# Row sums of a 64 MB array: the first 256 rows get a stretch of their own, and one semaphore guards the last store

## The chip, the core and the metric

The kernel runs on one core of a Trainium2 chip. The metric is the device time of one execution in microseconds (us), as the median over repeated runs. The engines that matter are DVE (VectorE), ACT (ScalarE), POOL (GpSimd) and SP (SyncE, which here issues every DMA); 16 DMA engines move the data. TensorE does no arithmetic here.

## The reference

```python
def setup_inputs():
    batch, seq, dim = 32, 512, 1024
    return {
        "x": np.random.randn(batch, seq, dim).astype(np.float32),
        "divisor": float(dim),
    }

def reference(x, divisor):
    return (np.sum(x, axis=-1) / divisor).astype(np.float32)
```

So x is 16,384 rows of 1,024 float32 (4 KB a row, 67.1 MB in all), and the output is one float32 per row, 64 KB.

## The kernel before

The rows are spread over the 128 partitions of the on-chip memory, 128 rows per partition. Three stretches of x are told apart, each with its own pattern of addresses. `x_first` is the start of x: 128 x 15 rows, where partition p owns 15 rows that follow one another, so that the whole stretch is packed. Behind it every partition owns W = 113 consecutive rows: the first M = 97 of them are `x_main`, the last L = 16 are `x_last`. Neighbouring partitions stand 113 rows (452 KiB) apart there.

The loads go, in this order, into three buffers `bulk0` to `bulk2` in turn (rows per partition, and in brackets how many of them ACT sums; DVE sums the others):

| load | 0 | 1 to 5 | 6 | 7 | 8 | 9 | then |
|---|---|---|---|---|---|---|---|
| stretch | main | main | main | first | last | last | last |
| rows | 2 (0) | 16 (0) each | 15 (4) | 15 (6) | 10 (4) | 4 (1) | 2, as `pa` and `pb` |

The lists in the code are `main = [(2, 0)] + [(16, 0)] * 5 + [(15, 4)]`, `first = [(15, 6)]` and `last = [(10, 4), (4, 1)]`. The last two rows come as `pa` (one and a half rows, 768 KB) and `pb` (half a row, 256 KB), so that little is left to add when the last bytes land.

DVE sums a load of `main` or `first` with one `reduce_sum` (L189), unscaled; ACT adds its rows one by one, with an activation that also gives the row's sum (L164). For `last`, DVE adds the two halves of a row with one custom instruction that scales and sums as well (`both_halves`, L180), and ACT scales in its activation. POOL scales the sums of `main` (L152) and `first` (L156) by 1/divisor afterwards. Sums stand in `res` (main), `res0` (first) and `fin` (last), and each of the three is stored by a DMA of its own.

The order is written out by hand. SP's first three loads (L111) are moved ahead of the program's opening barrier by `start_loads_at_once`. Each later bulk load (L138) waits until DVE and ACT are done with the buffer that it will overwrite, and until the load before it in that buffer has landed (L137). Then follow `pa` (L140) and `pb` (L141), the store of `res` (L143, after POOL's scaling), the store of `res0` (L145, likewise), and at the very end the store of `fin` (L205), which waits for ACT's count of rows and for DVE's count of instructions, two semaphores. The queue then waits for the two earlier stores, clears the semaphores (L210) and waits for the last store to land (L211). All DMAs stand in one queue, in the order of issue.

Of the kernel before, what the change touches and what calls it, by code (L numbers as in the profile page):

```python
# [9 lines left out]
COPY = mybir.ActivationFunctionType.Copy  # L10
# [24 lines left out]
@with_exitstack  # L35
def kernel(
    ctx: ExitStack,
    tc: tile.TileContext,
    x: bass.AP,
    divisor: float,  # L40
    out: bass.AP,
):
    nc = tc.nc
    nc.at_finalize(start_loads_at_once)
    xf = x.flatten_outer_dims()
    N, D = xf.shape
    P = nc.NUM_PARTITIONS
    scale = 1.0 / float(divisor)
    J = N // P
    assert J * P == N  # L50

    F, L = 15, 16
    M = J - F - L
    W = M + L
    x_first = bass.AP(tensor=x.tensor, offset=0, ap=[[F * D, P], [D, F], [1, D]])
    x_main = bass.AP(tensor=x.tensor, offset=P * F * D, ap=[[W * D, P], [D, M], [1, D]])
    x_last = bass.AP(tensor=x.tensor, offset=P * F * D + M * D, ap=[[W * D, P], [D, L], [1, D]])
    o_first = bass.AP(tensor=out.tensor, offset=0, ap=[[F, P], [1, F]])
    o_main = bass.AP(tensor=out.tensor, offset=P * F, ap=[[W, P], [1, M]])
    o_last = bass.AP(tensor=out.tensor, offset=P * F + M, ap=[[W, P], [1, L]])  # L60

    def room(name, *shape):
        return nc.alloc_sbuf_tensor(name, [P, *shape], F32).ap()


    base = -(-nc.sbuf_base // 32) * 32
    room("pad", -base % 1024 // 4)
    assert nc.sbuf_base % 1024 == 0
    c = 512
    bulk = [room(f"bulk{i}", r, D) for i, r in enumerate((16, 16, 16))]  # L70
    pa = room("pa", D + c)
    pb = room("pb", D - c + 16)[:, : D - c + 2]
    res0 = room("res0", F)
    res = room("res", M)
    fin = room("fin", L)
    junk = [nc.alloc_psum_tensor(f"junk{i}", [P, D], F32).ap() for i in range(4)]

    loads = []  # L80
    sems = {}

    def sem(name):
        sems[name] = nc.alloc_semaphore(name)
        return sems[name]

    in_bulk = [sem(f"in_bulk{i}") for i in range(3)]
    in_pa, in_pb = (sem(f"in_{n}") for n in ("pa", "pb"))
    out_first, out_main = sem("out_first"), sem("out_main")
    dve, act, pool = sem("by_dve"), sem("by_act"), sem("by_pool")  # L90
    landed = nc.alloc_semaphore("landed")

    n = 0
    main = [(2, 0)] + [(16, 0)] * 5 + [(15, 4)]
    first = [(15, 6)]
    last = [(10, 4), (4, 1)]
    assert sum(r for r, _ in first) == F
    assert sum(r for r, _ in main) == M and sum(r for r, _ in last) == L - 2
    for part, src, dst, by in (
        (main, x_main, res, 1.0), (first, x_first, res0, 1.0), (last, x_last, fin, scale)  # L100
    ):
        j = 0
        for rows, on_act in part:
            t, s, slot = bulk[n % 3][:, :rows, :], in_bulk[n % 3], n
            n += 1
            loads.append((t, s, src[:, j : j + rows, :], on_act, dst[:, j : j + rows], by, slot))
            j += rows


    for t, s, src, *_ in loads[:3]:  # L110
        i = nc.sync.dma_start(out=t, in_=src).then_inc(s, 16)  # L111
        tc.no_tile_sem_insts.add(i.ins.name)
    tc.close()
    tc.compile()  # L114


    done_dve, done_act = {}, {}
    d = a = 0
    for k, (t, s, src, on_act, dst, by, slot) in enumerate(loads):
        rows = t.shape[1]  # L120
        d += 1 if by == 1.0 else rows - on_act
        a += on_act
        done_dve[k], done_act[k] = d, a
    arrived, seen = [], {}
    for t, s, *_ in loads:
        seen[s.num] = seen.get(s.num, 0) + 16
        arrived.append(seen[s.num])


    for k, (t, s, src, on_act, dst, by, slot) in enumerate(loads):  # L130
        if k < 3:
            continue
        if slot is not None:
            nc.sync.wait_ge(dve, done_dve[k - 3])
            if done_act[k - 3]:
                nc.sync.wait_ge(act, done_act[k - 3])
            nc.sync.wait_ge(s, arrived[k] - 16)  # L137
        nc.sync.dma_start(out=t, in_=src).then_inc(s, 16)  # L138
    x_two = bass.AP(tensor=x.tensor, offset=x_last.offset + (L - 2) * D, ap=[[W * D, P], [1, 2 * D]])
    nc.sync.dma_start(out=pa, in_=x_two[:, : D + c]).then_inc(in_pa, 16)  # L140
    nc.sync.dma_start(out=pb[:, : D - c], in_=x_two[:, D + c :]).then_inc(in_pb, 16)  # L141
    nc.sync.wait_ge(pool, 2)
    nc.sync.dma_start(out=o_main, in_=res).then_inc(out_main, 16)  # L143
    nc.sync.wait_ge(pool, 3)
    nc.sync.dma_start(out=o_first, in_=res0).then_inc(out_first, 16)  # L145


    nc.gpsimd.memset(pb[:, D - c :], 0.0).then_inc(pool)  # L148
    k = len(main) - 1
    nc.gpsimd.wait_ge(dve, done_dve[k])  # L150
    nc.gpsimd.wait_ge(act, done_act[k])
    nc.gpsimd.tensor_scalar_mul(out=res, in0=res, scalar1=scale).then_inc(pool)  # L152
    k += len(first)
    nc.gpsimd.wait_ge(act, done_act[k])
    nc.gpsimd.wait_ge(dve, done_dve[k])
    nc.gpsimd.tensor_scalar_mul(out=res0, in0=res0, scalar1=scale).then_inc(pool)  # L156


    a = 0

    def row_on_act(src, by, dst):
        if a >= len(junk):
            nc.scalar.wait_ge(act, a - len(junk) + 1)
        nc.scalar.activation(junk[a % len(junk)], src, COPY, scale=by, accum_out=dst).then_inc(act)  # L164

    for k, (t, s, src, on_act, dst, by, slot) in enumerate(loads):
        rows = t.shape[1]
        for r in range(rows - on_act, rows):
            if r == rows - on_act:
                nc.scalar.wait_ge(s, arrived[k])  # L170
            row_on_act(t[:, r, :], by, dst[:, r : r + 1])
            a += 1
    nc.scalar.wait_ge(in_pa, 16)
    row_on_act(pa[:, :D], scale, fin[:, L - 2 : L - 1])
    a += 1


    def both_halves(dst, src, by):
        h = src.shape[-1] // 2
        return nc.vector.tensor_tensor_reduce(  # L180
            out=src[:, :h], in0=src[:, :h], in1=src[:, h:], scale=by, scalar=0.0,
            op0=ADD, op1=ADD, accum_out=dst,
        )

    for k, (t, s, src, on_act, dst, by, slot) in enumerate(loads):
        m = t.shape[1] - on_act
        nc.vector.wait_ge(s, arrived[k])
        if by == 1.0:
            nc.vector.reduce_sum(out=dst[:, :m], in_=t[:, :m, :], axis=AX).then_inc(dve)  # L189
        else:  # L190
            for r in range(m):
                both_halves(dst[:, r : r + 1], t[:, r, :], by).then_inc(dve)
    nc.vector.wait_ge(in_pa, 16)
    nc.vector.wait_ge(pool, 1)
    both_halves(pb[:, D - c : D - c + 1], pa[:, D:], 1.0).then_inc(dve)
    d += 1
    nc.vector.wait_ge(in_pb, 16)
    nc.vector.wait_ge(dve, d)
    both_halves(fin[:, L - 1 :], pb, scale).then_inc(dve)
    d += 1  # L200


    nc.sync.wait_ge(act, a)
    nc.sync.wait_ge(dve, d)
    nc.sync.dma_start(out=o_last, in_=fin).then_inc(landed, 16)  # L205
    for s in (out_first, out_main):
        nc.sync.wait_ge(s, 16)
    ids = [s.num for s in sems.values()]
    assert max(ids) - min(ids) + 1 == len(ids)
    nc.sync.sem_clear(range(min(ids), max(ids) + 1))  # L210
    nc.sync.wait_ge(landed, 16).then_inc(landed, -16)  # L211
# [35 lines left out]
```

## Time and profile before

| | |
|---|---|
| median of 3 runs | 160.44 us (160.41 to 160.47) |
| the profiled execution | 160.41 us, of which the traced span is 159.1 us |
| DVE busy | 116.5 us (73%) |
| ACT busy | 18.5 us (12%) |
| POOL busy | 1.0 us (1%) |
| DMA queue | 2160 packets, 67.18 MB, 98.1% of 16 engines' span, mean 422 GB/s |

The profile is of one execution. In the timeline a line gives start, duration, engine, source line and operation, and in brackets how long the engine had been idle and what ended that. A DVE or ACT line whose idle time ended with a DMA tells when that load landed. In the table of windows each line is a stretch of time with the busy time of DVE, ACT and POOL, the granted TensorE clock, the mean busy share of the DMA engines and GB/s; packets are counted where they start, so a short window can show more than the engines can move. In the table of DMA issues the last number is the time from issue to landing.

### The profile page before, as it was taken

The numbers are of one execution on the slowest core, as the hardware profiler recorded it, in microseconds if no ns is written. First come the engines' busy times: TensorE is split into PE (matmuls) and PEld (weight loads), VectorE is DVE, ScalarE is ACT, GpSimd is POOL, SyncE is SP. The second block draws the span as 40 slices with busy tenths as digits, with TensorE's granted clock in tenths as the row PEclk, the third lists the DMA queues.
The fourth block names the chain that finished last, engine by engine and source line by source line (L and its number), as shares of the span: only waits on it lengthen the run. The fifth ranks groups of instructions, "written<-read, shape, count | busy, mean of one in ns | idle before, by whom it ended". The sixth has DMA issues, their size and how long they took to land.

```text
span 159.1 us, 141 instructions
## 1 busy us (share of the span) xinstructions
DVE 116.5 (73%) x30; ACT 18.5 (12%) x33; POOL 1.0 (1%) x7
## 2 busy tenths in 40 slices
DVE  0500009999499994999949999599989990399475
ACT  3000000000000000000000000000009100392384
POOL 0000000000000000000000000000000001000000
DMA  8996996996997989969969969959996999798994
GB/s 330 461 527 264 527 527 264 527 527 264 527 478 313 527 363 428 527 264 527 527 264 527 527 264 527 494 247 494 494 494 278 463 494 494 330 453 371 420 400 152
DMA packets 2160, 67.18 MB, mean 422 GB/s; under 512 B 624, under 2 KB 624, under 8 KB 880
## 3 DMA queue, kind: packets, MB, share of 16 engines
q1 hardware_dynamic: 2160, 67.18, 98.1%
HBM read 67.11 MB, written 0.07 MB: 422 GB/s over the span
## 4 chain that ended last, share of the span: by engine, by line
DMA 67%; DVE 29%; another core or an unknown queue 1%; ACT 1%; SPq 1%; issue 0%
DMA bulk<-in_x_dram 51%; DVE res L189 29%; DMA pa<-in_x_dram 15%; ACT junk L164 1%; SPq L111 1%; SPq L138 0%
## 5 line engine op out<-in xcount | busy, mean ns | idle before, releaser
L189 DVE TENSOR_REDUCE res<-bulk 128x16 f32<-128x16384 f32 (+3 forms) x8 | 110.0, 13753 | 37.4 <-DMA bulk<-in_x_dram 37.4
L164 ACT ACTIVATE junk<-bulk 128x1024 f32<-128x1024 f32 x15 | 15.2, 1012 | 136.0 <-DMA bulk<-in_x_dram 136.0
L180 DVE CUSTOM_DVE_ANT_0 bulk<-bulk 128x512 f32<-128x512 f32 x9 | 5.7, 689 | 3.4 <-DMA bulk<-in_x_dram 3.4
L164 ACT ACTIVATION_READ_ACCUMULATOR junk<-bulk 128x1 f32 x15 | 2.8, 187 | 0.0
L164 ACT ACT_TABLE_LOAD x1 | 1.3, 1283 | 2.4 <-PEq L114 2.4
L152 POOL TENSOR_SCALAR res<-res 128x97 f32<-128x97 f32 x1 | 0.5, 465 | 128.9 <-DVE res L189 128.9
L164 ACT ACTIVATE junk<-pa 128x1024 f32<-128x1024 f32 x1 | 1.0, 1028 | 0.7 <-DMA pa<-in_x_dram 0.7
L180 DVE DVE_READ_ACCUMULATOR2_ANT fin<- 128x1 f32 x10 | 0.8, 83 | 0.0
L180 DVE CUSTOM_DVE_ANT_0 pb<-pb 128x257 f32<-128x257 f32 x1 | 0.4, 429 | 0.3 <-DMA pb<-in_x_dram 0.3
L180 DVE CUSTOM_DVE_ANT_0 pa<-pa 128x256 f32<-128x256 f32 x1 | 0.4, 426 | 0.0
L156 POOL TENSOR_SCALAR res<-res 128x15 f32<-128x15 f32 x1 | 0.3, 263 | 15.7 <-DVE res L189 15.7
L164 ACT ACTIVATION_READ_ACCUMULATOR junk<-pa 128x1 f32 x1 | 0.2, 186 | 0.0
L148 POOL MEMSET pb<- 128x2 f32 x1 | 0.1, 99 | 2.0 <-POOLq L114 2.0
L228 POOL MEMSET const-bfloat16-1.0<- 128x1 bf16 x1 | 0.1, 101 | 0.0
L228 POOL MEMSET const-uint8-127<- 128x1 uint8 x1 | 0.1, 101 | 0.0
L228 POOL MEMSET const-float32-0.0<- 128x1 f32 x1 | 0.1, 99 | 0.2 <-issue 0.2
L228 POOL MEMSET const-float32-1.0<- 128x1 f32 x1 | 0.1, 98 | 0.0
L180 DVE DVE_READ_ACCUMULATOR2_ANT pb<- 128x1 f32 x1 | 0.1, 83 | 0.0
## 6 DMA issues: line engine op xcount, KB each, us to landing
bulk<-in_x_dram SPq DMA_DIRECT2D x2, 7680.0 KB, 38.9
bulk<-in_x_dram SPq DMA_DIRECT2D x1, 5120.0 KB, 31.1
bulk<-in_x_dram SPq DMA_DIRECT2D x1, 2048.0 KB, 23.2
bulk<-in_x_dram SPq DMA_DIRECT2D x1, 1024.0 KB, 4.6
pa<-in_x_dram SPq DMA_DIRECT2D x1, 768.0 KB, 24.6
pb<-in_x_dram SPq DMA_DIRECT2D x1, 256.0 KB, 24.9
bulk<-in_x_dram SPq DMA_DIRECT2D x5, 40.8
out_dram<-res SPq DMA_DIRECT2D x1, 48.5 KB, 24.6
```

The lines of the kernel that those rows point to most:

```text
L111: i = nc.sync.dma_start(out=t, in_=src).then_inc(s, 16)
L148: nc.gpsimd.memset(pb[:, D - c :], 0.0).then_inc(pool)
L152: nc.gpsimd.tensor_scalar_mul(out=res, in0=res, scalar1=scale).then_inc(pool)
L156: nc.gpsimd.tensor_scalar_mul(out=res0, in0=res0, scalar1=scale).then_inc(pool)
L164: nc.scalar.activation(junk[a % len(junk)], src, COPY, scale=by, accum_out=dst).then_inc(act)
L180: return nc.vector.tensor_tensor_reduce(out=src[:, :h], in0=src[:, :h], in1=src[:, h:], scale=by, scalar=0.0, op0=ADD, op1=ADD, accum_out=dst,
L189: nc.vector.reduce_sum(out=dst[:, :m], in_=t[:, :m, :], axis=AX).then_inc(dve)
L228: nc = _bacc.Bacc("TRN2", target_bir_lowering=False, num_devices=1)
```

## The change

A fourth stretch, `x_begin`, is cut off the start of x: G = 2 rows per partition, 256 rows, packed in 1 MB. It takes the place of the two rows of `main` that were loaded first; `first` (15 rows per partition, packed) follows it in memory, and `main` and `last` are now 95 + 16 = 111 rows per partition. The order and the sizes of the loads remain: 2, five times 16, 15, 15, 10, 4 rows, `pa`, `pb`.

The two rows of `begin` are summed on DVE by `both_halves`, scaled at once, into a tile of their own, `res1`, which gets a store of its own, issued right after that of `res0`. POOL scales 95 columns of `res` in place of 97.

A semaphore `done` counts the last instruction of ACT and the last of DVE; the last store waits for it alone to reach 2. The queue's closing waits take in the new store.

```diff
-    F, L = 15, 16
-    M = J - F - L
+    G, F, L = 2, 15, 16
+    M = J - G - F - L
     W = M + L
-    x_first = bass.AP(tensor=x.tensor, offset=0, ap=[[F * D, P], [D, F], [1, D]])
-    x_main = bass.AP(tensor=x.tensor, offset=P * F * D, ap=[[W * D, P], [D, M], [1, D]])
+    x_begin = bass.AP(tensor=x.tensor, offset=0, ap=[[G * D, P], [D, G], [1, D]])
+    x_first = bass.AP(tensor=x.tensor, offset=P * G * D, ap=[[F * D, P], [D, F], [1, D]])
+    x_main = bass.AP(tensor=x.tensor, offset=P * (G + F) * D, ap=[[W * D, P], [D, M], [1, D]])
...
+    o_begin = bass.AP(tensor=out.tensor, offset=0, ap=[[G, P], [1, G]])
...
+    res1 = room("res1", G)
     res = room("res", M)
...
-    main = [(2, 0)] + [(16, 0)] * 5 + [(15, 4)]
+    begin = [(2, 0)]
+    main = [(16, 0)] * 5 + [(15, 4)]
...
-        (main, x_main, res, 1.0), (first, x_first, res0, 1.0), (last, x_last, fin, scale)
+        (begin, x_begin, res1, scale), (main, x_main, res, 1.0),
+        (first, x_first, res0, 1.0), (last, x_last, fin, scale),
...
     nc.sync.dma_start(out=o_first, in_=res0).then_inc(out_first, 16)
+    nc.sync.dma_start(out=o_begin, in_=res1).then_inc(out_begin, 16)
...
-    row_on_act(pa[:, :D], scale, fin[:, L - 2 : L - 1])
-    a += 1
+    row_on_act(pa[:, :D], scale, fin[:, L - 2 : L - 1], done)
...
-    both_halves(fin[:, L - 1 :], pb, scale).then_inc(dve)
-    d += 1
-    nc.sync.wait_ge(act, a)
-    nc.sync.wait_ge(dve, d)
+    both_halves(fin[:, L - 1 :], pb, scale).then_inc(done)
+    nc.sync.wait_ge(done, 2)
     nc.sync.dma_start(out=o_last, in_=fin).then_inc(landed, 16)
-    for s in (out_first, out_main):
+    for s in (out_begin, out_first, out_main):
         nc.sync.wait_ge(s, 16)
```

More of the change, by code (lines that the diff above doesn't have):

```diff
@@ L50 @@
     assert J * P == N
-    F, L = 15, 16
-    M = J - F - L
+    G, F, L = 2, 15, 16
+    M = J - G - F - L
     W = M + L
-    x_first = bass.AP(tensor=x.tensor, offset=0, ap=[[F * D, P], [D, F], [1, D]])
-    x_main = bass.AP(tensor=x.tensor, offset=P * F * D, ap=[[W * D, P], [D, M], [1, D]])
[L57 to L60, printed above, removed]
+    x_begin = bass.AP(tensor=x.tensor, offset=0, ap=[[G * D, P], [D, G], [1, D]])
+    x_first = bass.AP(tensor=x.tensor, offset=P * G * D, ap=[[F * D, P], [D, F], [1, D]])
+    x_main = bass.AP(tensor=x.tensor, offset=P * (G + F) * D, ap=[[W * D, P], [D, M], [1, D]])
+    x_last = bass.AP(tensor=x.tensor, offset=P * (G + F) * D + M * D, ap=[[W * D, P], [D, L], [1, D]])
+    o_begin = bass.AP(tensor=out.tensor, offset=0, ap=[[G, P], [1, G]])
+    o_first = bass.AP(tensor=out.tensor, offset=P * G, ap=[[F, P], [1, F]])
+    o_main = bass.AP(tensor=out.tensor, offset=P * (G + F), ap=[[W, P], [1, M]])
+    o_last = bass.AP(tensor=out.tensor, offset=P * (G + F) + M, ap=[[W, P], [1, L]])
     def room(name, *shape):
@@ L88 @@
     in_pa, in_pb = (sem(f"in_{n}") for n in ("pa", "pb"))
-    out_first, out_main = sem("out_first"), sem("out_main")
+    out_begin, out_first, out_main = (sem(f"out_{n}") for n in ("begin", "first", "main"))
     dve, act, pool = sem("by_dve"), sem("by_act"), sem("by_pool")
+    done = sem("done")
     landed = nc.alloc_semaphore("landed")
     n = 0
-    main = [(2, 0)] + [(16, 0)] * 5 + [(15, 4)]
+    begin = [(2, 0)]
+    main = [(16, 0)] * 5 + [(15, 4)]
     first = [(15, 6)]
@@ L145 @@
     nc.sync.dma_start(out=o_first, in_=res0).then_inc(out_first, 16)
+    nc.sync.dma_start(out=o_begin, in_=res1).then_inc(out_begin, 16)
     nc.gpsimd.memset(pb[:, D - c :], 0.0).then_inc(pool)
-    k = len(main) - 1
+    k = len(begin + main) - 1
     nc.gpsimd.wait_ge(dve, done_dve[k])
@@ L159, with row_on_act @@
     a = 0
-    def row_on_act(src, by, dst):
+    def row_on_act(src, by, dst, count):
         if a >= len(junk):
             nc.scalar.wait_ge(act, a - len(junk) + 1)
-        nc.scalar.activation(junk[a % len(junk)], src, COPY, scale=by, accum_out=dst).then_inc(act)
+        nc.scalar.activation(junk[a % len(junk)], src, COPY, scale=by, accum_out=dst).then_inc(count)
     for k, (t, s, src, on_act, dst, by, slot) in enumerate(loads):
@@ L170 @@
                 nc.scalar.wait_ge(s, arrived[k])
-            row_on_act(t[:, r, :], by, dst[:, r : r + 1])
+            row_on_act(t[:, r, :], by, dst[:, r : r + 1], act)
             a += 1
     nc.scalar.wait_ge(in_pa, 16)
-    row_on_act(pa[:, :D], scale, fin[:, L - 2 : L - 1])
-    a += 1
+    row_on_act(pa[:, :D], scale, fin[:, L - 2 : L - 1], done)
     def both_halves(dst, src, by):
```

## The prediction

> **What bounds the kernel now.** I read the page first, then the timeline for the moments at which loads land, then windows over the start, then the end of the timeline and the queue's own waits. The page:
>
> ```profile
> span 159.1 us, 141 instructions
> DVE 116.5 (73%) x30; ACT 18.5 (12%) x33; POOL 1.0 (1%) x7
> q1 hardware_dynamic: 2160, 67.18, 98.1%
> DMA 67%; DVE 29%; another core or an unknown queue 1%; ACT 1%; SPq 1%; issue 0%
> ```
>
> The transfers are busy 98.1% of the span on one queue. The chain of waits names DVE for 29%, but that share is misleading: a chain followed back from the end may pass through a reduction that merely frees a buffer for a load that then stands in line. The timeline settles it:
>
> ```profile
> 0.00 1.32 SPq L111 DMA_DIRECT2D bulk<-in_x_dram  x3
> 4.65 2.29 DVE L189 TENSOR_REDUCE res<-bulk 128x2 f32<-128x2048 f32 x1 [4.65 <-DMA bulk<-in_x_dram]
> 6.96 124.72 SPq L138 DMA_DIRECT2D bulk<-in_x_dram  x7
> 23.95 17.22 DVE L189 TENSOR_REDUCE res<-bulk 128x16 f32<-128x16384 f32 x1 [17.02 <-DMA bulk<-in_x_dram]
> 43.29 17.22 DVE L189 TENSOR_REDUCE res<-bulk 128x16 f32<-128x16384 f32 x1 [2.12 <-DMA bulk<-in_x_dram]
> ...
> 119.44 11.89 DVE L189 TENSOR_REDUCE res<-bulk 128x11 f32<-128x11264 f32 x1 [0.90 <-DMA bulk<-in_x_dram]
> ...
> 137.66 9.75 DVE L189 TENSOR_REDUCE res<-bulk 128x9 f32<-128x9216 f32 x1 [6.33 <-DMA bulk<-in_x_dram]
> ```
>
> Every reduction waits for its load, never the other way round. From 4.65 to 119.44 five loads of 16 rows and one of 15 land: 95 rows per partition in 114.79 us, 1.208 us a row. A row of all partitions is 128 x 4096 = 524,288 bytes, so this is 434 GB/s. The packed load of 15 rows (119.44 to 137.66) needs 18.22 us, 1.215 us a row. With three buffers the queue always holds a load in waiting, and a 16-row reduction (17.22) is shorter than its load (19.33), so there is no gap to close between 4.65 and the end. What can move is the start, the price of a row, and the last 2 us.
>
> The start, by windows (the last two columns are the DMA share and GB/s, counted where packets start):
>
> ```profile
> 0.00:1.00 1.00, 0.00 (x0) 0.00 (x0) 0.19 (x4) 1.00 0.06 8
> 1.00:2.00 1.00, 0.00 (x0) 0.00 (x0) 0.00 (x0) 1.00 0.86 221
> 2.00:3.00 1.00, 0.00 (x0) 0.61 (x1) 0.10 (x1) 1.00 0.99 418
> 3.00:3.90 0.90, 0.00 (x0) 0.67 (x1) 0.00 (x0) 1.00 1.01 428
> ```
>
> Data begin to move at about 1.0 us, but in the first microsecond of moving they go at half speed although the engines count as 86% busy: the first packets last long. Against 434 GB/s the loss is (1 - 221/434) = 0.49 us, then 0.04 and 0.01: 0.54 us in all, and everything behind in the queue stands that much later.
>
> The end, and what the queue waits for there:
>
> ```profile
> 157.12 0.43 DVE L180 CUSTOM_DVE_ANT_0 pb<-pb 128x257 f32<-128x257 f32 x1 [0.27 <-DMA pb<-in_x_dram]
> 157.37 0.19 ACT L164 ACTIVATION_READ_ACCUMULATOR junk<-pa 128x1 f32 x1
> 157.47 0.08 DVE L180 DVE_READ_ACCUMULATOR2_ANT fin<- 128x1 f32 x1
> 157.63 0.33 SPq L205 DMA_DIRECT2D out_dram<-fin  x1
> ```
> ```profile
> L204 SPq EVENT_SEMAPHORE  x1: 17/17/17, 157.6 to 157.6; - x1
> out_dram<-fin SPq DMA_DIRECT2D x1, 8.0 KB, 1.4
> ```
>
> DVE ends at 157.55 and ACT at 157.56, the store is issued at 157.63, lands 1.4 later, and that is the end of the span (159.1). The profiled execution took 160.41 us as a whole, 1.3 around its span; the median of the runs is 160.44, so 0.03 is added to sums made on it.
>
> **The change part by part.**
>
> *Where the first load reads.* Both versions load two rows per partition first, into the same buffer, in pieces of 8 KB. Before, the 128 pieces stand 113 rows (452 KiB) apart, all over x; after, they close up to 1 MB. Bytes, pieces and issue are the same, so only the loss of 0.54 us at the start is open to it. The most it can give is -0.54. On the other side, the packed megabyte could move at the start's slow 221 GB/s from end to end: 1.05 MB would take 4.75 us instead of the roughly 2.96 that 2.42 at full speed and the loss make up, +1.8. The nearest row for packed addresses is the load of 15 rows: 1.215 us a row against 1.208, so packing costs next to nothing once the stream runs (2 rows x 0.007 = 0.01 us). The slow microsecond is different: it is the first reading of x, at places scattered over all of it, and these addresses are the one thing that the change alters there. I take -0.32, some 60% of the loss; this is a choice between the ends, not a measured value.
>
> [...]
>
> *Cold addresses behind it.* The 16-row loads no longer follow pieces that the first load has touched. If first touch were what is slow, the loss might move to the second load. But the 15-row load reads a stretch that nothing had read before and loses 15 x 0.007 = 0.1 us at most. I take 0, with 0 to +0.1.
>
> *Pitch 113 becomes 111 rows*, for the 111 rows of each partition that follow it. The bulk runs at 1.208 us a row; bounded by the slowest row price seen, 1.215, this costs 0 to 111 x 0.0065 = +0.7. The two prices come from very different pitches (452 and 60 KiB) and are 0.5% apart, so I take 0. A gain below 1.208 has its nearest row in the 4-row load (149.75 to 154.56: 1.203), -0.6 for all; its ends are blurred by two landings, so it counts for little.
>
> *DVE's first work.* One reduction of 2.29 becomes two combined adds with their read-outs, by the later rows 2 x 0.61 = 1.2 from start to start. It runs at 4.65 and DVE then has nothing until 23.95. SP's issue of the fourth load moves from 6.96 to about 5.9, but this load stands behind two others until 43. Cost 0; the cover is 17 us of idle DVE and 36 us of queue. POOL's scaling of 97 columns becomes 95: 0.47 us at 131.4, beside loads.
>
> *The added store* of 8 bytes per partition follows the 15-row store on SP, so about 0.34 us of issue at 148.2. SP has then nothing to issue until 157.6, and no load stands behind it. Only the last store does. The 15-row store is issued at 147.86, lands 9.7 us later at 157.5, behind the loads; the last store's whole way of 1.4 begins at 157.63. A small store landing by 157.8 to 158 costs nothing, since the queue's closing wait for the last store lasts to 159.1. If the eight-byte pieces held the last store up, the bound is the whole issue-to-landing time of such a store, 1.4. I take 0, with 0 to +0.3 in the range, as its packets are an eighth of the last store's bytes.
>
> [...]
>
> *One wait instead of two.* Between DVE's end (157.55) and the issue (157.63) lie 0.08 us, with the separate wait L204 (17 ns) in them. With one semaphore the wait rides on the store itself. The chain of waits has a pair without such a step in between:
>
> ```profile
> 131.34 0.02 issue
> 131.36 0.33 SPq L138
> ```
>
> So the 0.08 can shrink by 0.02 (the wait alone) to 0.06 (down to this 0.02); I take -0.04. The added wait for the third store is between 158.0 and 159.1, under the landing: 0. Nothing else is queued behind it.
>
> Sum: 160.41 - 0.32 - 0.04 = 160.05; with 0.03 to the median, 160.08.
>
> **The rivals.**
>
> *The start keeps its loss (same).* If the slow microsecond belongs to the first reads as such, wherever they go, only the tail moves: 160.44 - 0.04 = 160.40. For it: 86% busy at half the bytes looks like waiting on a cold path. Against: the packets recover within a microsecond, unevenly. It is also the case in which the change does nothing of what it says, since the two rows came first already.
>
> *The packed megabyte starts worse (slower).* All engines read one small stretch at once, in step. Place: windows 1 to 4 us. Price: up to +1.8, the half-way value +0.9 gives 161.3. It decides from the point where the first landing is later than about 5.0 us, 0.36 over 4.65, as the tail gives 0.04 back. Against it: the packed 15-row load lost only 0.5%.
>
> *The stream pays for the pitch of 111 (slower).* 111 rows at the packed load's price: +0.7, 161.1. It decides when a 16-row load takes 0.05 us more than 19.33. Against it: two unlike pitches 0.5% apart.
>
> **How the numbers follow.** About 0.2%, 0.32 us, is what a measurement of this kernel can tell from no change. Chances: the start gains 0.50 (159.88 to 160.24, of which 0.45 lies below 160.12); the start keeps its loss 0.27 (160.30 to 160.55); packed start worse 0.13; pitch 0.10. So faster 0.45, same 0.32, slower 0.23. The likeliest case's own range is 159.88 to 160.24. The range of 8 in 10 runs from 159.85, the whole 0.54 and the tail, to 160.9, which takes in the case of no change, the small store's 0.3 and the mild part of the slower rivals, and leaves their far part out.
>
> **What would show it.** Right: the first reduction starts near 4.3 instead of 4.65, the window 1:2 moves well over 221 GB/s, later landings stay 19.3 apart, and the last store is issued some 0.04 after DVE's end. Wrong: the first landing at 4.6 or later, or landings of 16 rows 19.4 or more apart, or a last store that takes over 1.5 from issue to landing.

## The result, and the profile after

The changed kernel takes 162.89 us (median of 6 runs, 162.05 to 163.09) against 160.45 us for the kernel before: a ratio of 1.0136, 95% interval 1.0120 to 1.0151. It is slower by a little over 2 us; the forecast was 160.08, in a range of 159.85 to 160.9. The profiled execution took 162.05 us and is the shortest of the six, so its lines show the smallest form of the loss; its span is 160.7 us against 159.1.

The timeline of the changed kernel at the places shown of before:

```profile
0.00 1.34 SPq L117 DMA_DIRECT2D bulk<-in_x_dram  x3
4.83 0.69 DVE L186 CUSTOM_DVE_ANT_0 bulk<-bulk 128x512 f32<-128x512 f32 x1 [4.83 <-DMA bulk<-in_x_dram]
...
24.11 17.22 DVE L195 TENSOR_REDUCE res<-bulk 128x16 f32<-128x16384 f32 x1 [17.97 <-DMA bulk<-in_x_dram]
43.44 17.22 DVE L195 TENSOR_REDUCE res<-bulk 128x16 f32<-128x16384 f32 x1 [2.11 <-DMA bulk<-in_x_dram]
...
148.48 0.45 SPq L152 DMA_DIRECT2D out_dram<-res  x1
...
157.35 0.43 DVE L186 CUSTOM_DVE_ANT_0 pb<-pb 128x257 f32<-128x257 f32 x1 [0.26 <-DMA pb<-in_x_dram]
...
157.83 0.33 SPq L209 DMA_DIRECT2D out_dram<-fin  x1
```

The first landing is 0.18 later than before (4.83 against 4.65), a 16-row load still takes 19.33, and the last store is issued 0.20 later (157.83 against 157.63). So far only 0.2 of the 1.6 us in the span is found. The rest stands in the table of DMA issues (the last column is the time from issue to landing; the 1.0 KB line is the new store) and in the queue's own waits:

```profile
out_dram<-res SPq DMA_DIRECT2D x1, 47.5 KB, 26.1
out_dram<-res SPq DMA_DIRECT2D x1, 7.5 KB, 11.7
out_dram<-res SPq DMA_DIRECT2D x1, 1.0 KB, 11.5
out_dram<-fin SPq DMA_DIRECT2D x1, 8.0 KB, 2.9
```
```profile
SPq L211 <- DMA out_dram<-res: 1.7, 1, 1.7
```

The last store lands 2.9 us after its issue in place of 1.4. The two older stores land later too, although both stand ahead of the new store in the queue: the first now takes 26.1, the second 11.7. Their lines before:

```profile
out_dram<-res SPq DMA_DIRECT2D x1, 48.5 KB, 24.6
out_dram<-res SPq DMA_DIRECT2D x1, 7.5 KB, 9.7
```

And the queue now waits 1.7 us at L211, which in this kernel is the closing wait for the earlier stores; before, it cost nothing. The new store itself, 128 pieces of 8 bytes issued at 148.48, lands 11.5 later, at about 160.0. Sum for the span: 0.20 up to the issue and 2.86 - 1.42 = 1.44 behind it, 1.64.

### The profile page after: what moved, and what is told of

Its sections match the earlier page's. It is cut to its first block, busy times and chain, and to the rows that moved or that the text cites. A ratio compares the mean times of both kernels' runs of the same rounds, so it can differ in the third digit from the quotient of the medians.

```text
span 160.7 us, 144 instructions
## 1 busy us (share of the span) xinstructions
DVE 115.5 (72%) x33; ACT 18.5 (11%) x33; POOL 1.0 (1%) x7
## 4 chain that ended last, share of the span: by engine, by line
DMA 66%; DVE 29%; another core or an unknown queue 1%; ACT 1%; SPq 1%; issue 0%
DMA bulk<-in_x_dram 51%; DVE res L195 29%; DMA pa<-in_x_dram 15%; ACT junk L171 1%; SPq L117 1%; SPq L144 0%
## 5 line engine op out<-in xcount | busy, mean ns | idle before, releaser
L195 DVE TENSOR_REDUCE res<-bulk 128x16 f32<-128x16384 f32 (+2 forms) x7 | 107.7, 15391 | 33.8 <-DMA bulk<-in_x_dram 33.8
L186 DVE CUSTOM_DVE_ANT_0 bulk<-bulk 128x512 f32<-128x512 f32 x11 | 7.0, 689 | 8.2 <-DMA bulk<-in_x_dram 8.2
L159 POOL TENSOR_SCALAR res<-res 128x95 f32<-128x95 f32 x1 | 0.5, 462 | 129.1 <-DVE res L195 129.1
## 6 DMA issues: line engine op xcount, KB each, us to landing
out_dram<-res SPq DMA_DIRECT2D x1, 47.5 KB, 26.1
```

The source lines that it names most:

```text
L186: return nc.vector.tensor_tensor_reduce(out=src[:, :h], in0=src[:, :h], in1=src[:, h:], scale=by, scalar=0.0, op0=ADD, op1=ADD, accum_out=dst,
```

## The experiments

**Without the new store.** The theory after the first look: the 8-byte pieces of the new store hold up the last one. Rivals: the packed start or the pitch of 111 rows; the new waits.

```diff
-    nc.sync.dma_start(out=o_begin, in_=res1).then_inc(out_begin, 16)
...
-    for s in (out_begin, out_first, out_main):
+    for s in (out_first, out_main):
```

> This is the changed kernel without the store of res1; the 256 sums of the first stretch are not written. Theory A (the 8-byte pieces of that store, eight to a run of 64 bytes, hold back the last store's landing): the last store lands again about 1.4 us after its issue (2.86 in the changed kernel), and the time falls to the time of the kernel before plus the later first landing (4.83 against 4.65) less the merged wait: 160.5 to 160.7. Theory B (packed start or pitch 111 make the loss): it stays at 162 or above. Theory C (the merged wait or the extra closing wait makes it): it stays at 162 or above as well.

Measured: 160.93 us, ratio 1.0025 (1.0014 to 1.0036), and the last store lands as before:

```profile
out_dram<-fin SPq DMA_DIRECT2D x1, 8.0 KB, 1.4
```

Some four fifths of the loss go with the store. A remainder of 0.4 us stays on this chip, more than the 160.5 to 160.7 expected; it is taken up below.

**The store moved to where nobody waits for it.** It is issued after the fourth load and so stands in the queue between that load and the next.

> The changed kernel with the store of res1 issued right after the fourth load (about 6.5 us) and not after the store of res0. Theory A: the same 128 pieces of 8 bytes go through between two loads at about 43 us, where nobody waits for them; the last store lands in about 1.4 us, and the time is that of the kernel without this store, within 0.3 us (the pieces may stall loads behind them by up to some 0.3): 160.5 to 161.0. Rival A2 (the pieces stall the engines wherever they stand, so the loads behind them come 1 to 2 us later): the landing of the fourth load (62.85 in the changed kernel) moves to 64 or later and the time stays at 162 or more. Theories B and C: 162 or more.

Measured: 163.93 us, ratio 1.0209 (1.0194 to 1.0224), slower still. The landings of the fourth and fifth loads in the timeline of this kernel:

```profile
62.94 17.22 DVE L196 TENSOR_REDUCE res<-bulk 128x16 f32<-128x16384 f32 x1 [2.19 <-DMA bulk<-in_x_dram]
85.24 17.22 DVE L196 TENSOR_REDUCE res<-bulk 128x16 f32<-128x16384 f32 x1 [5.08 <-DMA bulk<-in_x_dram]
```

Between them lie 22.30 us, where every other 16-row load takes 19.3: the kilobyte costs about 3 us of the whole stream, as much as 1.3 MB of loads. Rival A2 was right. At the end of the kernel a part of the same hold-up falls between the last load's landing and the last store's start, where the last sums run anyway; in the stream nothing covers it. The last store landed in 1.4 us again.

**Is it the 8 bytes?** The kernel before, with two columns of `res` stored apart:

```diff
-    nc.sync.dma_start(out=o_main, in_=res).then_inc(out_main, 16)
+    nc.sync.dma_start(out=o_main[:, 2:], in_=res[:, 2:]).then_inc(out_main, 16)
...
     nc.sync.dma_start(out=o_first, in_=res0).then_inc(out_first, 16)
+    nc.sync.dma_start(out=o_main[:, :2], in_=res[:, :2]).then_inc(out_begin, 16)
```

> The kernel before, with the sums of its first load (2 columns of res) taken out of the store of res and stored apart, right after the store of res0: 128 pieces of 8 bytes as in the changed kernel, but 452 bytes from one to the next instead of next to one another. Theory A1 (what hurts is that eight pieces fall into the same 64 bytes, or all into the same 1 KB): no hold-up, the last store lands 1.4 to 1.5 us after its issue, the time is 160.4 to 160.7. Theory A2 (a piece of 8 bytes is costly wherever it lies): hold-up as in the changed kernel, landing after 2.5 to 3.5 us and a time of 162 to 163.

Measured: 160.67 us, ratio 1.0006 (0.9997 to 1.0016), and in the table of DMA issues (the first line is the store of the two columns):

```profile
out_dram<-res SPq DMA_DIRECT2D x1, 1.0 KB, 9.7
out_dram<-fin SPq DMA_DIRECT2D x1, 8.0 KB, 1.4
```

Pieces of 8 bytes as such cost nothing that can be told from nothing. The same split made in `res0`, so that the pieces stand 60 bytes apart:

> The kernel before with the store of res0 (15 columns) split: 13 columns as before, and 2 columns as 128 pieces of 8 bytes that stand 60 bytes apart, about one to each 64-byte line, in 7.5 KB, next to the other store's pieces. If the hold-up needs several pieces in one run of 64 bytes, none is seen: last store landing 1.4 us after issue, time 160.4 to 160.8. If it needs only that the pieces crowd into a few KB, or that two stores write into the same lines, a hold-up appears: landing 2 us or more, time over 161.5.

Measured: 160.56 us, ratio 1.0002 (0.9993 to 1.0012), last landing 1.4. Neither a few KB full of pieces nor two stores that share lines is enough.

**How the hold-up grows.** Half of the pieces, `o_begin[:64]` and `res1[:64]`, and twice as many, one store for each column:

> The changed kernel with the store of res1 cut to partitions 0 to 63: 64 pieces of 8 bytes in 512 bytes, still eight to each 64 bytes (the sums of the other 128 rows are not written). If the pieces of one 64-byte line go one after another and lines go side by side, half the lines cost as much as all: the hold-up remains, last store landing 2.5 us or more, time 162 to 163. If all 128 pieces go one after another (the early store took 65.8 - 62.7 = 3.1 us for 128, 24 ns each), half of them cost half: a hold-up of 1.5 us from about 156.8, ended before the last store's pieces start at 158.6, landing 1.4 to 1.8 and a time of 160.8 to 161.3.

> The changed kernel with the store of res1 split into two stores of one column: 256 pieces of 4 bytes for the same 1 KB, so twice as many per line and in all. Both forms of Theory A1 expect the hold-up to double from some 3 us to some 6: last store landing 5 to 6.5 us after issue, time 164.5 to 166.5. If the cost went by bytes, or by lines touched, it would stay at 162 to 163.

Measured: the half 162.2 us, ratio 1.0089 (1.0056 to 1.0122), last landing 2.1; the double 165.98 us, ratio 1.0343 (1.0310 to 1.0377), last landing:

```profile
out_dram<-res SPq DMA_DIRECT2D x2, 0.5 KB, 13.7
out_dram<-res SPq DMA_DIRECT2D x1, 7.5 KB, 15.1
out_dram<-fin SPq DMA_DIRECT2D x1, 8.0 KB, 6.6
```

(The two new stores share a semaphore, so the 13.7 is not the landing of both.) The double came nearly as expected, its time within the 164.5 to 166.5, its landing just over the 6.5. How long a store holds up is seen best in the trace's semaphore updates of the new store, sixteen to a DMA: from the first to the last they take 2.0 us with 64 pieces, 2.8 with 128 and 6.4 with 256, so the double holds up more than twice as long, with the same bytes and the same lines. The half fell between the two expectations (162 to 163 and 160.8 to 161.3 were foretold; the median is in the first, the profiled execution of 161.27 in the second), so these two don't decide whether lines go side by side; a later run has more on it.

**What counts: the size of a piece, or how many share a line?** With G = 4 the pieces are 16 bytes, four to a run of 64:

```diff
-    G, F, L = 2, 15, 16
+    G, F, L = 4, 15, 16
...
-    begin = [(2, 0)]
-    main = [(16, 0)] * 5 + [(15, 4)]
+    begin = [(4, 0)]
+    main = [(16, 0)] * 4 + [(14, 0), (15, 4)]
```

> The changed kernel with G = 4: a packed first load of 4 rows per partition (2 MB), 93 + 16 rows behind, and a store of 128 pieces of 16 bytes next to one another (2 KB, four to each 64 bytes). If all pieces of such a store go one after another, 128 of them hold up as long as in the changed kernel (2.8 us from first to last semaphore update in the profile): last landing 2.5 us or more, time 162.5 to 163.3. If what counts is how many share a line (4 in place of 8), the hold-up halves to some 1.4 us and is nearly over when the last store starts: landing 1.4 to 1.9, time 160.8 to 161.5.

Measured: 160.88 us, ratio 1.0021 (1.0012 to 1.0031), and:

```profile
out_dram<-res SPq DMA_DIRECT2D x1, 2.0 KB, 9.9
out_dram<-fin SPq DMA_DIRECT2D x1, 8.0 KB, 1.4
```

As many pieces, and the last store isn't held up. That alone leaves open whether the hold-up is gone or, as the expectation has it, halved and over in time. On this kernel, only some of the columns are stored, or the columns in two stores:

```diff
-    nc.sync.dma_start(out=o_begin, in_=res1).then_inc(out_begin, 16)
+    nc.sync.dma_start(out=o_begin[:, :2], in_=res1[:, :2]).then_inc(out_begin, 16)      # e15_8B_pitch16
...
+    for r in (0, 2):                                                                    # e16_8B_twice
+        nc.sync.dma_start(out=o_begin[:, r : r + 2], in_=res1[:, r : r + 2]).then_inc(out_begin, 16)
...
+    nc.sync.dma_start(out=o_begin[:, :1], in_=res1[:, :1], allow_slow_non_contiguous=True).then_inc(out_begin, 16)    # e17_4B_pitch16
```

> The kernel of e11_16B_pieces (first load of 4 rows, 128 pieces of 16 bytes, no hold-up), storing only two of the four columns: 128 pieces of 8 bytes, 16 bytes from one to the next, four to each 64 bytes; half of the first stretch's sums are not written. If the number of pieces per line decides (eight hold up, four do not), no hold-up: landing 1.4 to 1.5, time as e11_16B_pieces, 160.7 to 161.1. If the size of a close piece decides (8 bytes hold up, 16 do not), landing 2.5 or more and 162 to 163.

> The kernel of e11_16B_pieces with its store in two of two columns each: 256 pieces of 8 bytes, each store four to a 64-byte line, both together eight to a line, all sums written. If eight pieces per line decide even across two stores, hold-up about as in the changed kernel: landing 2.5 or more, 162 or more. If the count per line within one store decides, none: 160.7 to 161.2.

> The kernel of e11_16B_pieces storing one column of four: 128 pieces of 4 bytes, 16 bytes apart, four to a 64-byte line; three quarters of the first stretch's sums are not written. Pieces per line: no hold-up, 160.7 to 161.1. Size of a close piece: hold-up, 162 or more.

Measured: 8 bytes at a pitch of 16: 161.0 us, ratio 1.0030 (1.0019 to 1.0041), last landing 1.5. 4 bytes at a pitch of 16: 160.98 us, ratio 1.0028 (1.0018 to 1.0037), last landing 1.4. Two stores of 8-byte pieces on the same lines: 162.89 us, ratio 1.0141 (1.0122 to 1.0160), and in the table of DMA issues:

```profile
out_dram<-res SPq DMA_DIRECT2D x2, 1.0 KB, 10.6
out_dram<-res SPq DMA_DIRECT2D x1, 7.5 KB, 12.3
out_dram<-fin SPq DMA_DIRECT2D x1, 8.0 KB, 3.1
```

So with four pieces to each 64 bytes the last store lands as before, at 4, 8 and 16 bytes a piece; eight hold it up, from one store or from two; sixteen far longer. It is the crowding of pieces into one short run of memory, not their size. The 0.3 to 0.5 us by which the three kernels with four to a run stand above the kernel before lie ahead of the last store: in their profiles it is issued at 157.97 to 158.29 in place of 157.63, and the first load, of four rows here, landed at 7.57 to 7.92. The kernel with two stores has such a part too: its last store is issued at 158.60, so of the 2.6 us in its span 1.0 stand ahead of the issue and 1.65 behind it.

Four to a run are not wholly without price. From the first to the last semaphore update the new store takes 0.8 us with pieces 60 or 452 bytes apart, 0.9 with 16-byte pieces, 1.5 and 1.6 with 8 and 4 bytes at a pitch of 16, 2.8 in the changed kernel, and the two stores together 4.0; 0.4 to 1.2 of each is there already in the updates of the last load. The cost grows with the crowding, and up to four it ends early enough that the last store's landing doesn't show it. The two stores also bear on the lines. At eight to a run, 64, 128 and 256 pieces take 2.0, 2.8 and 4.0 from first to last update: more runs cost more, but far less than in proportion, while 256 pieces at sixteen to a run take 6.4. So the runs go neither one after another nor wholly side by side. That the run is 64 bytes long is the unit in which I counted; a shorter or longer one was not told apart.

**The store mended.** If crowding is the cause, larger pieces cure it. The two rows of partition p become rows p and 128 + p, and DVE turns the sums so that 32 of them lie in a row:

```diff
+    nc.vector.transpose(out=turned, in_=res1).then_inc(zero)
...
-    nc.sync.dma_start(out=o_begin, in_=res1).then_inc(out_begin, 16)
+    for r in range(G):
+        nc.sync.dma_start(out=o_begin[r], in_=turned[r::32, :]).then_inc(out_begin, 16)
```

> The changed kernel with its store mended: the two rows of partition p in the first load are rows p and 128 + p of x (pieces of 4 KB from the same packed 1 MB), DVE turns the 128 x 2 sums by blocks of 32 x 32 at about 6 us, and the store of the first stretch is two DMAs of 4 pieces of 128 bytes. Every sum is written. Theory A1: no hold-up, last landing 1.4 to 1.5 us after issue, and the time is that of the changed kernel without the store, 160.7 to 161.2, so still over the kernel before for the packed start. If the hold-up belongs to any third small store in the tail, it remains at 162 or more.

Measured: 160.66 us, ratio 1.0007 (0.9997 to 1.0016), last landing 1.5. The changed kernel without its loss, and no faster than the kernel before.

**The start.** The kernel before, its first load reading the packed megabyte, and then one with a pitch of 512 KiB:

```diff
+    x_packed = bass.AP(tensor=x.tensor, offset=0, ap=[[2 * D, P], [D, 2], [1, D]])    # 128 * D for the second
...
-        i = nc.sync.dma_start(out=t, in_=src).then_inc(s, 16)
+        i = nc.sync.dma_start(out=t, in_=x_packed if n == 0 else src).then_inc(s, 16)
```

> The kernel before with one edit: the first load reads the packed first megabyte of x, as in the changed kernel, in place of two rows of x_main; the sums of 256 rows are therefore those of other rows. Pitch, stores and waits are those of before. If the packed addresses are what makes the first landing late, the first reduction starts at about 4.83 in place of 4.65, all later landings shift by that, and the time is 160.55 to 160.75. If it is the pitch of 111 or chance, the first landing stays at 4.65 and the time at 160.45. My prediction's step (the packed start gains 0.32) would need 4.33 and 160.1.

> The kernel before with the first load reading two rows of every 128 (pitch 512 KiB; the sums of 256 rows are therefore those of other rows). [...] If only the first microsecond depends on the addresses, as in the packed start (first landing 4.87 and 0.3 us on the median), the landing stays within 4.4 to 5.2 and the time within 160.2 to 161.0.

Measured: packed 160.75 us, ratio 1.0021 (1.0010 to 1.0032), first landing 4.87; 512 KiB 160.66 us, ratio 1.0010 (1.0000 to 1.0019), first landing 4.91. The first looks as if packing cost 0.3 us. But the kernels with the old, scattered first load landed it at 4.61 (e1_one_wait), 4.86 (e5_spread_8B) and 4.94 (e10_pitch_60B), each on another chip. Two kernels on one chip, different in the first load's addresses alone, settle it for that chip:

> The changed kernel without the store of res1 (as in e2_no_begin_store), and with its first load reading two rows of every 111 (the first two of each partition's stretch of x_main) in place of the packed megabyte; 256 sums are not written. Pitch 111, DVE's halves and the one wait stay. If packing is what costs the remaining 0.3 to 0.4 us, the ratio to the kernel before falls to 0.999 to 1.0005. If the pitch of 111 costs it, the ratio stays at 1.002 or above.

> The kernel of e2_no_begin_store beside e13_spread_start on one chip, so that the two differ in the addresses of the first load alone. If packing costs, it stands 0.2 to 0.4 us above e13_spread_start, with a ratio of about 1.0025 to the kernel before, and in the profile its first landing is the later one by about 0.2. If the first landing belongs to the chip (the same scattered load landed at 4.61, 4.86 and 4.94 in profiles of three chips), the two are alike within 0.1.

Measured: spread 160.60 us, ratio 1.0006 (0.9997 to 1.0015), packed 160.58 us, ratio 1.0006 (0.9997 to 1.0015). The first landings, spread and then packed:

```profile
4.99 0.69 DVE L185 CUSTOM_DVE_ANT_0 bulk<-bulk 128x512 f32<-128x512 f32 x1 [4.99 <-DMA bulk<-in_x_dram]
```
```profile
4.87 0.69 DVE L185 CUSTOM_DVE_ANT_0 bulk<-bulk 128x512 f32<-128x512 f32 x1 [4.87 <-DMA bulk<-in_x_dram]
```

On this chip packing costs nothing and gains nothing that shows, and the pitch of 111, which both have, costs at most 0.24 us, the upper end of the interval. The same kernel stood at 1.0025 on the chip of e2_no_begin_store, and the kernel before with the packed load at 1.0021 (e4_packed_start). What differs in the profiles is the scattered load: the packed two rows in pieces of 8 KB landed at 4.83 to 4.88 in all seven profiles that have them, the scattered ones at 4.61 on that chip, at 4.86, 4.94 and 4.99 on three others and at 4.65 in the profile of the kernel before. With one profile of each kernel it isn't shown that the chip makes this. Nor is the start all of it: in the profile of e2_no_begin_store the last store is issued 0.84 later than before, of which 0.18 stand at the first landing and about half come with the last two loads.

**The one wait.**

> The kernel before with the last store waiting for the one semaphore alone, as in the changed kernel. The prediction's term: -0.02 to -0.06, so 160.38 to 160.43, with the store issued 0.03 to 0.06 after DVE's end in place of 0.08. Theory C (the one wait costs something) would give over 160.6. In the changed kernel's profile DVE ends at 157.78 and the store is issued at 157.83, 0.05, which speaks for the first.

Measured: 160.46 us, ratio 0.9994 (0.9985 to 1.0004); in its profile the store is issued at 157.56, 0.05 after DVE's end at 157.51 and 0.03 after ACT's at 157.53, against 0.08 and 0.07 before. The 0.03 to 0.04 us are there in the profile and too small for the times. No version tried was faster than the kernel before beyond doubt.

## Why the prediction was wrong

*The step that failed* is "The added store": I took 0, allowed 0.3 in the range and called 1.4 the bound. It measured 1.44 in the profiled execution, and between 1.8 and 2.1 by the ratios (1.0136 with the store, 1.0025 and 1.0006 without it on two chips, each times 160.5). Three errors are in that step. I sized the store by its bytes ("an eighth of the last store's bytes"), where the runs show that it goes by how many pieces crowd into one run of memory. My nearest row, the 7.5 KB store, has pieces of 60 bytes next to one another, about one to each 64 bytes; the new store has eight, so the row wasn't near in what mattered. And the issue-to-landing time of a small store is no bound for what it does to others: two columns of 4 bytes made the last store's landing 6.6. Of the signs of being wrong that I had named, two came: a first landing at 4.6 or later, and a last store that takes over 1.5 from issue to landing.

The Trainium skill, page "DMA: Bandwidth & Descriptors", section Specifications, says that transfers below 512 bytes make the DMA engine read, modify and write. That rule speaks against all stores of this kernel alike (pieces of 380, 60, 64 and 8 bytes); the runs show no price of 8-byte pieces that stand 60 or 452 bytes apart (ratios 1.0002 and 1.0006), and a hold-up when they crowd, which the rule doesn't say. A queue of such cycles on one line would fit the hold-up, but no run shows them.

*What stands behind the store.* I wrote that only the last store does. That was right, and the reason why the early place is dearer: there the loads stand behind it, 3 us by the timeline. But I looked for the delay on the new store's own landing, by 157.8 to 158 where it was 160.0, and took the last store's delay for a mere bound. The stores ahead of it also landed later, by 1.5 and 2.0 us in the profile.

*The start*, taken at -0.32, gave nothing. The first landing was later, not earlier: 4.83. On the chip of e13_spread_start the addresses make no difference, on another the packed ones cost 0.3. The slow first microsecond is there for all addresses of the two rows: in the window 1:2 the packed 8 KB pieces move at 123 to 213 GB/s, the scattered ones at 180 to 221, and a pitch of 512 KiB at 172, with its first landing at 4.91. So it isn't the scattering of the first reads; my rival "the start keeps its loss" held on the one chip, and on the other packing cost a little on top.

*Right in size:* the one wait (0.03 to 0.04 in the profile for the 0.04 taken); DVE's first work (SP's fourth load moved from 6.96 to 6.17, and its landing stayed hidden); 16-row landings 19.33 apart; the pitch of 111 at no price that shows. The rivals on the slower side were the wrong ones: neither named the store, whose price I had shut out of the chances with a small number in the range.

## What to carry to other kernels

A store of a few bytes per partition that closes up in memory costs by how many pieces fall into one short run: here four to 64 bytes cost the end of the kernel nothing, eight cost it about 2 us and the middle of a stream 3 us, sixteen cost the end over 5 us. Turn or join such results on chip into longer pieces, or store them within a wider row, before they leave. And an edge of a DMA-bound kernel is not free just because its engines idle there: ask what the DMA engines hold when the last store comes.

## What the runs showed of the hardware that I had not expected

One kilobyte in 128 adjacent pieces of 8 bytes delays a stream of loads over 16 DMA engines by about 3 us (landings 22.30 apart in place of 19.3), and stores ahead of it in the same queue land up to 2.0 us later as well. The identical first load, two rows at a pitch of 113, lands between 4.61 and 4.94 us in profiles of different chips, a scatter as large as the whole gain that I had forecast for it.
